# First mixer pass on unnormalized operands, with its outputs scaled, the weight folds inside the pass, and two reorderings

## The chip, the cores and the metric

One core of a Trainium2 chip runs the whole kernel. The metric is the device time of one execution in microseconds (us); smaller is better. The engines are TensorE (PE, with its weight load PEld), VectorE (DVE), ScalarE (ACT), GpSimd (POOL) and SyncE (SP, which here issues the DMA transfers).

## The reference

The kernel computes two layers over a sequence of 2048 rows of 1024 channels, in float32. Layer 0 mixes with a gated short convolution, layer 1 with causal window means in four groups; after each mixer comes a gated embedding of `p`, and one norm ends it.

```
def rmsnorm(x, g):
    r = lax.rsqrt(jnp.mean(xf * xf, axis=-1, keepdims=True) + EPS)
    return (xf * r) * g
def short_conv_mixer(h, w_in, w_conv, w_out):
    b_g, c_g, v, z = jnp.split(h @ w_in, 4, axis=-1)
    y = b_g * causal_conv3(c_g * v, w_conv)
    return (jax.nn.silu(z) * y) @ w_out
def pool_mixer(h, w_in, w_grp, scale, w_out):
    u, z = jnp.split(h @ w_in, 2, axis=-1)
    d = pooled - u4                      # causal means over 2, 4, 8, 16 rows, by group
    mixed = einsum('bsgc,gcd->bsgd', d, w_grp) * scale
    return (jax.nn.silu(z) * mixed) @ w_out
def reference(...):
    for i in range(DEPTH):               # DEPTH = 2
        hn = rmsnorm(h, norm_mix[i])
        h = h + mixer(hn, ...)           # i = 0: short_conv_mixer, i = 1: pool_mixer
        gate = sigmoid(rmsnorm(h, ple_norm[i]) @ ple_w_gate[i])
        h = h + gate * (p[i] @ ple_w_proj[i])
    return rmsnorm(h, final_norm)
```

## The kernel before

**Tiles.** Channels lie on the 128 partitions (8 tiles, `KT`), the sequence along the free dimension in four chunks of `T` = 512 rows. A pass (`sc`) takes two chunks through all stages, so there are two passes. `x` arrives twice in memory: `xT` with channels on partitions, `xN` with rows on partitions.

**Products.** A float32 product is made of three in a shorter form: weights and operands are each split into a high part (a cast on ACT: L116 for weights, L301 for operands) and the rest (a subtraction on DVE: L117, L302). The three matmuls are L273, L274 and L275, of 512 columns each. Operands that need only a channel gain are split by L307 (ACT) and L308 (DVE).

**The pair scheme.** In the mixers two chunks and two weight blocks are multiplied by seven products in place of eight. `Operands` holds the seven operand combinations (x11, x21, t2, t1, t3, x22, t4; four tiles each, 28 splits of 128x512); `pair_steps` is a generator of four steps (parts 0 to 3), whose PSUM results are copied by ACT (L428) and added by DVE (L433). `mixer_a` runs 8 output blocks `j`, each with a `cv` pair (the c and v projections) and a `zb` pair (z and b): 2 x 7 products of 12 matmuls, 168 matmuls per `j`. From c and v comes `u` (L484, DVE), then the convolution (one scale on ACT, L491, two DVE steps, L493, for each chunk), then sigmoid (L511), L512, L513 and `y` (L516).

**Weights.** They come in granules of 128x1024 (512 KB): `order` is the list of them as they will be asked for, `load_granule` issues the DMA on SP (L110) into `raw` (4 buffers), ACT and DVE split it into a weight ring (4 buffers), and `prefetch` keeps up to `LOOK` = 3 ahead (1 in the start). In the first pass the scheme's weight sums (L134 to L140 on DVE) are also written to memory, and `prepare_sums` makes those of the output weights (L548 on `n` tiles); the second pass loads them. Other pools: `wk` 10 tiles of 128x512 for elementwise work, `pm` 7 PSUM tiles, `acts` 31.

**The start.** The order in the program is: load chunk 0 of `xT`; sums of squares of chunk 0 (`square_sums`: ACT L328, DVE L331); the embedding products of chunks 0 and 1 (`ple_half`, 96 matmuls; each result is copied by ACT at L735 and stored by L736 to `pdr`); load chunk 1; `roots`; `fold` for groups 0 and 1 (a product of `w_grp` with the output weights, 48 matmuls of 256 columns for a group, 192 in all); squares of chunk 1 on PE with a matrix of ones (L879); the operands x11, x21 with their norm (`normed`, L545: gain and row factor `rb` in one DVE instruction); `fold` for groups 2 and 3; t2. Then `mixer_a` begins.

**The turn.** Between the passes, at the gates of layer 1, `X.ahead(1 + t)` splits operands of the second pass (their tiles `n` come back from memory, `ndr`), once after each gate block; `finals` writes outputs, and `filler` makes the embedding products of chunk 2 (eight L735 copies).

**What sets the order.** A scheduler fixes each engine's order when the program is built, by priority in program order; every engine then runs its list in order, and an instruction that waits holds up all behind it on its engine. The lines of `mixer_a` that the change touches:

```
cs1, cs2, v1, v2 = pair_of(cv_steps)
...                                    # u = c * v, then cv = conv(u)
z1, z2, b1, b2 = pair_of(zb_steps)     # takes the steps that are left
if j + 1 < KT:
    cv_steps = steps(j + 1, 0)
    next(cv_steps)
```

## Time and profile before

| what | value |
|---|---|
| median of 3 runs | 1846.69 us (1844.87 to 1856.14) |
| the profiled execution | 1848.54 us, its span 1846.8 us |
| mean granted TensorE clock | 0.991 of full speed |
| PE busy | 1776.5 us (96%), 8014 instructions |
| DVE busy | 1350.7 us (73%), 1878 instructions |
| ACT busy | 754.6 us (41%), 1141 instructions |
| POOL busy | 233.3 us (13%), 218 instructions |
| from memory, to memory | 225.49 MB, 97.52 MB |

The span counts from the first to the last instruction; 1.7 us of the profiled execution lie around it. The profiled execution is 1.9 us above the median. Busy matmuls overlap in the records, so a PE that is shown busy need not be at its full pace; the count of matmuls in a stretch says what it did.

### The profile page before, as it was taken

The page shows a single profiled execution, that of the slowest core. Times are in us where ns is not written, and L with a number is a line of the kernel's source. Part 1 is how long each engine was busy: PE and PEld are TensorE (multiplying, and loading weights), DVE is VectorE, ACT ScalarE, POOL GpSimd, SP SyncE. Part 2 cuts the span into 40 slices and gives each one's busy share as a digit, 9 for nine tenths or more (in the row PEclk, how much of TensorE's full clock was granted, in tenths as well). Part 3 has the DMA queues.
Part 4 walks back from the last instruction along what each step waited for, and adds up shares of the span by engine and source line. Part 5 has one row for each costly group of instructions (what it writes and reads, how often), then busy time and mean ns, then how long its engine had stood idle before and what let it go on. Part 6 is the DMA issues. An engine that isn't in the chain of part 4 may idle for free.

```text
span 1846.8 us, 22147 instructions
## 1 busy us (share of the span) xinstructions
PE 1776.5 (96%) x8014; PEld 1459.0 (79%) x8014; DVE 1350.7 (73%) x1878; ACT 754.6 (41%) x1141; POOL 233.3 (13%) x218
## 2 busy tenths in 40 slices
PE   8799999989999999999979999999999999999996
PEld 6587777878788888887868877877878888888796
DVE  4886776776988778879786555466698876578975
ACT  6642333344656221345553233234465511135542
POOL 1000000000322010013210000000032300001320
PEclk9999999999999999999999999999999999999998
DMA  9545455667355456853674434246635522265431
GB/s 322 191 146 195 168 205 186 243 232 272 114 194 187 146 198 221 281 198 127 209 239 155 137 103 137 94 146 221 246 126 194 192 109 99 97 224 170 142 114 47
DMA packets 122495, 324.49 MB, mean 176 GB/s; under 512 B 13584, under 2 KB 15632, under 8 KB 122384
## 3 DMA queue, kind: packets, MB, share of 16 engines
q1 hardware_dynamic: 122384, 323.06, 50.8%
q8 instruction: 63, 1.03, 0.2%
q14 instruction: 48, 0.39, 0.1%
HBM read 225.49 MB, written 97.52 MB: 175 GB/s over the span
## 4 chain that ended last, share of the span: by engine, by line
PE 65%; DVE 17%; issue 5%; DMA 5%; ACT 3%; POOL 1%; SPq 1%; DVEq 0%; ACTq 0%; POOLq 0%
PE mm L275 22%; PE mm L273 21%; PE mm L274 21%; DVE w L117 5%; DVE act L302 2%; DMA n<-ndr 2%; DMA n<-in_wts_dram 2%; DVE act L308 2%; ACT w L116 1%; DVE h L699 1%; DMA raw<-in_wts_dram 1%; DVE wk L754 1%; DVE n L548 1%; SPq L601 1%; ACT wk L428 1%
## 5 line engine op out<-in xcount | busy, mean ns | idle before, releaser
L273 PE MATMUL mm<-act,w 128*128 128x512 f32 (+1 forms) x2464 | 942.2, 385 | 19.5 <-ACT wk L428 10.8
L275 PE MATMUL mm<-act,w 128*128 128x512 f32 (+1 forms) x2464 | 935.0, 384 | 12.2 <-DVE w L117 12.0
L274 PE MATMUL mm<-act,w 128*128 128x512 f32 (+1 forms) x2464 | 943.7, 383 | 0.0
L273 PEld LDWEIGHTS mm<-act,w 128*128 128x128 f32 x2464 | 464.2, 188 | 121.3 <-ACT wk L428 16.6
L275 PEld LDWEIGHTS mm<-act,w 128*128 128x128 f32 x2464 | 463.2, 188 | 108.4 <-DVE w L117 17.7
L274 PEld LDWEIGHTS mm<-act,w 128*128 128x128 f32 x2464 | 464.4, 188 | 90.5 <-issue 0.5
L116 ACT CAST w<-raw 128x1024 fp32r<-128x1024 f32 (+1 forms) x283 | 281.6, 1002 | 563.2 <-PE mm L275 474.7
L117 DVE TENSOR_TENSOR w<-raw,w 128x1024 fp32r<-128x1024 f32 (+1 forms) x283 | 336.6, 1194 | 130.8 <-ACT w L116 127.2
L331 POOL TENSOR_TENSOR acc<-acc,wk 128x512 f32<-128x512 f32 x97 | 142.9, 1474 | 490.4 <-ACT wk L328 490.4
L433 DVE TENSOR_TENSOR wk<-mm,wk 128x512 f32<-128x512 f32 x96 | 65.8, 686 | 100.5 <-PE mm L275 100.5
L308 DVE SCALAR_TENSOR_TENSOR act<-h,par_sb,act 128x512 fp32r<-128x512 f32 x96 | 103.8, 1084 | 19.9 <-ACT act L307 17.9
L328 ACT ACTIVATE wk<-h 128x512 f32<-128x512 f32 (+1 forms) x126 | 75.3, 600 | 93.6 <-DVE h L755 93.2
L307 ACT ACTIVATE act<-h,par_sb 128x512 fp32r<-128x512 f32 x96 | 68.9, 718 | 72.7 <-DVE h L699 72.7
L699 DVE TENSOR_TENSOR h<-mm,h 128x512 f32<-128x512 f32 x112 | 75.9, 682 | 26.7 <-PE mm L275 20.7
L302 DVE TENSOR_TENSOR act<-n,act 128x512 fp32r<-128x512 f32 x112 | 76.3, 710 | 22.8 <-ACT act L301 22.7
L428 ACT COPY wk<-mm 128x512 f32<-128x512 f32 x96 | 53.0, 585 | 94.9 <-PE mm L275 94.9
L301 ACT CAST act<-n 128x512 fp32r<-128x512 f32 x112 | 65.7, 619 | 57.3 <-DMA n<-ydr 27.6
L669 DVE TENSOR_TENSOR wk<-wk 128x526 f32<-128x526 f32 (+5 forms) x80 | 55.5, 693 | 2.4
L352 POOL TENSOR_TENSOR r<-ms,nhalf 128x8 f32<-128x8 f32 x18 | 33.1, 1837 | 186.5 <-DVE ms L350 186.5
L684 ACT ACTIVATE wk<-wk 128x512 f32<-128x512 f32 x32 | 20.2, 630 | 78.0 <-DVE wk L682 77.9
L753 ACT ACTIVATE wk<-wk 128x512 f32<-128x512 f32 (+1 forms) x72 | 41.3, 579 | 21.6 <-DVE wk L752 21.4
L682 DVE TENSOR_TENSOR wk<-mm,rb 128x512 f32<-128x512 f32 x32 | 22.0, 688 | 37.6 <-PE mm L275 37.6
(124 smaller groups left out, 1296.1 us busy)
## 6 DMA issues: line engine op xcount, KB each, us to landing
raw<-in_wts_dram SPq DMA_DIRECT2D x154, 512.0 KB, 3.4
n<-ydr SPq DMA_DIRECT2D x84, 256.0 KB, 4.5
ydr<-y SPq DMA_DIRECT2D x32, 512.0 KB, 3.3
raw<-in_wts_dram SPq DMA_DIRECT2D x64, 256.0 KB, 3.3
raw<-sdo SPq DMA_DIRECT2D x32, 512.0 KB, 6.3
raw<-sda SPq DMA_DIRECT2D x32, 512.0 KB, 3.7
pdr<-wk SPq DMA_DIRECT2D x56, 256.0 KB, 4.0
n<-pdr SPq DMA_DIRECT2D x56, 256.0 KB, 3.5
```

Source lines behind the costliest of these rows:

```text
L116: nc.scalar.copy(out=hi[:, c], in_=raw[:, c])
L117: eng.tensor_tensor(out=lo[:, c], in0=raw[:, c], in1=hi[:, c].bitcast(F32), op=ALU.subtract)
L273: nc.tensor.matmul(out=ps, lhsT=wh, rhs=ah, start=first, stop=False, skip_group_check=skip)
L274: nc.tensor.matmul(out=ps, lhsT=wh, rhs=al, start=False, stop=False, skip_group_check=skip)
L275: nc.tensor.matmul(out=ps, lhsT=wl, rhs=ah, start=False, stop=last, skip_group_check=skip)
L302: nc.vector.tensor_tensor(out=a[:, 1, :], in0=y, in1=a[:, 0, :].bitcast(F32), op=ALU.subtract)
L307: nc.scalar.activation(out=a[:, 0, :], in_=h, func=AF.Copy, scale=pcol(gcol))
L308: nc.vector.scalar_tensor_tensor(out=a[:, 1, :], in0=h, scalar=pcol(gcol), in1=a[:, 0, :].bitcast(F32), op0=ALU.mult, op1=ALU.subtract)
L328: nc.scalar.activation(out=sq, in_=h, func=AF.Square)
L331: (eng or nc.gpsimd).tensor_tensor(out=acc, in0=acc, in1=sq, op=ALU.add)
L428: nc.scalar.copy(out=c, in_=ps)
L699: nc.vector.tensor_tensor(out=hs[t][k], in0=ps, in1=hs[t][k], op=ALU.add)
```

## The change

1. **The first pass runs on unnormalized operands.** They carry only the channel gains (`split_scaled`, and `gained`, which takes the place of a `normed` with a `vec`). The row factor is found by `row_stats(0)`: eight `xN` tiles of 512 KB are loaded, squared with an accumulating ACT instruction, and the factors are spread over the partitions by two matmuls. `rb` multiplies z and the convolution's result, and its square `rb2` multiplies c: six more DVE multiplications per `j`. The sums of squares, the roots and the products with ones at the start go.
2. **The folds** leave the start; `fold(g)` stands after the zb pair of `j` = 2, 3, 4, 5, and each loads three granules of its own.
3. **The z, b steps** (parts 0 and 1 of the zb pair) are asked for ahead of the convolution, in both passes.
4. **At the turn** `X.ahead(1)` stands in place of `X.ahead(1 + t)`: 16 of the 28 operands are split there, not 24.

The diff, cut:

```
--- before.py
+++ after.py
...
 HK = D // 2
+FOLDS = 3
 LAG = 3
...
+    def fold_order(g):
+        return [("w", W_GRP + g // 2), ("w", W_UT + 2 * g), ("w", W_UT + 2 * g + 1)]
     def sum_order(sc, n):
...
     order += ple_order(0, 0, "p", "pt") + [("p", 1)]
-    for g in range(4):
-        kind = "pt" if g < 2 else "w"
-        order += [("pt", W_GRP + g // 2)] if g % 2 == 0 else []
-        order += [(kind, W_UT + 2 * g), (kind, W_UT + 2 * g + 1)]
     for sc in range(2):
         order += filler_order(0, 2) if sc else []
-        order += sum_order(sc, 2 * KT)
+        order += sum_order(sc, 4)
+        for i in range(4, 2 * KT, 2):
+            order += fold_order(i // 2 - FOLDS) if sc == 0 and FOLDS <= i // 2 < FOLDS + 4 else []
+            order += [("sum", (sc, i + r, part)) for r in range(2) for part in range(4)]
         order += filler_order(0, 3) if sc else filler_order(1, 0)
...
-    def fold(g, wg, u):
+    def fold(g):
+        wg, *u = [next_granule(key) for key in fold_order(g)]
         for half in range(2):
...
                 look[0] = LOOK
+                if sc == 0:
+                    rb = list(row_stats(0))[-1]
+                    rb2 = []
+                    for t in range(2):
+                        rb2.append(rbp.tile([P, T], F32, tag="rb", name="rb2"))
+                        nc.scalar.activation(out=rb2[t], in_=rb[t], func=AF.Square)
             cs1, cs2, v1, v2 = pair_of(cv_steps)
...
                 u = wtile()
+                if sc == 0:
+                    vec(c, c, rb2[t], ALU.mult)
                 nc.gpsimd.tensor_copy(out=u[:, 0:2], in_=uh[:, j, :] if t == 0 else us[0][:, T:T + 2])
...
                 nc.gpsimd.tensor_copy(out=uh[:, j, :], in_=us[1][:, T:T + 2])
+            if j:
+                next(zb_steps)
+            next(zb_steps)
             cvs = []
...
             z1, z2, b1, b2 = pair_of(zb_steps)
+            if sc == 0 and FOLDS <= j + 1 < FOLDS + 4:
+                fold(j + 1 - FOLDS)
             if j + 1 < KT:
...
                 cv = cvs[t][:, :T]
+                if sc == 0:
+                    vec(z, z, rb[t], ALU.mult)
+                    vec(cv, cv, rb[t], ALU.mult)
                 zs = wtile()[:, :T]
...
-    def first_operand(x, stats):
+    def first_operand(x):
+        def gained(out, x, k, y, op):
+            nc.vector.scalar_tensor_tensor(out=out, in0=x, scalar=pcol(G_MIX + k), in1=y, op0=ALU.mult, op1=op)
         def make(name, kk):
-            n11, n12, n21, n22 = (x[t][2 * kk + r] for r in range(2) for t in range(2))
+            k1, k2 = 2 * kk, 2 * kk + 1
+            n11, n21 = x[0][k1], x[0][k2]
             if name == "x11":
-                normed(n11, n11, 2 * kk, stats[0].rb)
-                return split_act(n11)
+                return split_scaled(n11, G_MIX + k1)
             if name == "x21":
-                normed(n21, n21, 2 * kk + 1, stats[0].rb)
-                return split_act(n21)
+                return split_scaled(n21, G_MIX + k2)
+            n12, n22 = x[1][k1], x[1][k2]
+            if name == "x22":
+                return split_scaled(n22, G_MIX + k2)
             if name == "t2":
-                normed(n12, n12, 2 * kk, stats[1].rb)
-                normed(n22, n22, 2 * kk + 1, stats[1].rb)
-                vec(n12, n22, n12, ALU.subtract)
-                vec(n11, n12, n11, ALU.add)
-                return split_act(n11)
+                nc.scalar.activation(out=n12, in_=n12, func=AF.Copy, scale=pcol(G_MIX + k1))
+                gained(n12, n22, k2, n12, ALU.subtract)
+                gained(n11, n11, k1, n12, ALU.add)
             if name == "t1":
-                vec(n21, n21, n11, ALU.subtract)
-                vec(n11, n22, n11, ALU.subtract)
-                return split_act(n11)
-            return split_act({"t3": n12, "x22": n22, "t4": n21}[name])
+                gained(n21, n21, k2, n11, ALU.subtract)
+                gained(n11, n22, k2, n11, ALU.subtract)
+            return split_act({"t2": n11, "t1": n11, "t3": n12, "t4": n21}[name])
         return make
...
-    def square_sums(t):
...
-    def square_sums_pe(t):
...
-                nc.scalar.activation(out=sq[:, k - i, :], in_=x[t][k], func=AF.Square)
-                nc.tensor.matmul(out=tot, lhsT=ones_s, rhs=sq[:, k - i, :], start=k == 0, stop=k == KT - 1)
...
-    def roots(t):
...
-    def fold_next(g):
...
-    prefetch(2)
+    prefetch(3)
     load_chunk(0)
-    prefetch(3)
-    square_sums(0)
     pt = next_granule(("p", 0))
...
             pt = next_granule(("p", 1))
-    prefetch(8)
+    X = Operands(first_operand(x))
+    X("x11")
     load_chunk(1)
-    roots(0)
-    fold_next(0)
-    fold_next(1)
-    square_sums_pe(1)
-    X = Operands(first_operand(x, stats))
-    X("x11")
     X("x21")
-    fold_next(2)
-    fold_next(3)
     X("t2")
...
+    def row_stats(sc):
+        ssum = st.tile([P, 8], F32, tag="ssum", name="ssum")
+        for j in range(KT):
+            t = acts.tile([P, D], F32, tag="act", name="xr")
+            nc.sync.dma_start(out=t, in_=xN[sc * KT + j])
+            nc.scalar.activation(out=t, in_=t, func=AF.Square, accum_out=ssum[:, j:j + 1])
+            if j == KT - 1:
+                ms = st.tile([P, 8], F32, tag="ms8", name="ms8")
+                nc.vector.tensor_scalar(out=ms, in0=ssum, scalar1=1.0 / D, scalar2=EPS, op0=ALU.mult, op1=ALU.add)
+                r = st.tile([P, 8], F32, tag="r8", name="r8")
+                nc.gpsimd.tensor_tensor(out=r, in0=ms, in1=nhalf, op=ALU.pow)
+                yield spread(r, 0), spread(r, 4)
+            else:
+                yield
     rbs = []
+    row_steps = row_stats(1)
     def gather(j):
...
+        rbs.extend(next(row_steps) or ())
...
             if sc == 0:
-                X.ahead(1 + t)
+                X.ahead(1)
```

How this moves instructions, at three places. First SP's list in the start, in the embedding of chunk 1; `pdr_134` and `pdr_135` are stored embedding products, `h` is chunk 1 of `xT`, `s` and `sda` are weight sums and where they are stored, `xr` are the `xN` tiles. Before:

```order
L736 DMA pdr_134<-wk 128x512 x8
L736 DMA pdr_135<-wk 128x512 x3
L401 DMA h<-in_xT_dram 128x1024 x2
L736 DMA pdr_135<-wk 128x512 x3
L401 DMA h<-in_xT_dram 128x1024 x2
L736 DMA pdr_135<-wk 128x512 x2
L419 DMA wcomb_122<-wc 128x512
```

After:

```order
L759 DMA pdr_135<-wk 128x512
L404 DMA h<-in_xT_dram 128x1024 x2
L759 DMA pdr_135<-wk 128x512
L111 DMA raw<-in_wts_dram 128x1024
L183 DMA sda_145<-s_486 128x1024
L759 DMA pdr_135<-wk 128x512 x3
L187 DMA sda_145<-raw 128x1024
L759 DMA pdr_135<-wk 128x512 x3
L111 DMA raw<-in_wts_dram 128x1024
L909 DMA xr<-in_xN_dram 128x1024 x8
L111 DMA raw<-in_wts_dram 128x1024
```

The last two loads of chunk 1 stand behind nine stores (eight of `pdr_134` stand ahead of the rows shown) in place of fourteen, and the eight `xN` tiles behind all of these, behind the first stored sums and behind two granules of weights.

Second, ACT's list at the last `j` of the second pass; the casts of `w` split weights, those of `n` are operands of a later stage. Before:

```order
L301 CAST act<-n 128x512 x5
L116 CAST w<-raw 128x1024
L116 CAST w<-raw 128x512
L116 CAST w<-raw 128x1024
L491 ACTIVATE wk<-wk,par_sb 128x512 x2
L428 COPY wk<-mm 128x512 x3
L116 CAST w<-raw 128x1024 x2
L511 ACTIVATE wk<-wk 128x512 x2
L735 COPY wk<-mm 128x512
```

After:

```order
L304 CAST act<-n 128x512 x5
L117 CAST w<-raw 128x1024
L117 CAST w<-raw 128x512
L117 CAST w<-raw 128x1024
L432 COPY wk<-mm 128x512 x3
L506 ACTIVATE wk<-wk,par_sb 128x512 x2
L117 CAST w<-raw 128x1024 x2
L531 ACTIVATE wk<-wk 128x512 x2
```

The three PSUM copies (L428, now L432) now stand ahead of the two convolution scales (L491, now L506).

Third, ACT's list at the turn, at the first copies of the filler (L735, now L758); the casts of `n` are the splits of the second pass's operands, and L753 (L776) belongs to the gate. Before:

```order
L301 CAST act<-n 128x512
L328 ACTIVATE wk<-h 128x512
L301 CAST act<-n 128x512
L753 ACTIVATE wk<-wk 128x512
L301 CAST act<-n 128x512
L328 ACTIVATE wk<-h 128x512
L735 COPY wk<-mm 128x512 x4
L301 CAST act<-n 128x512 x2
```

After:

```order
L304 CAST act<-n 128x512 x2
L331 ACTIVATE wk<-h 128x512
L304 CAST act<-n 128x512
L776 ACTIVATE wk<-wk 128x512
L117 CAST w<-raw 128x1024
L304 CAST act<-n 128x512 x3
L331 ACTIVATE wk<-h 128x512
L758 COPY wk<-mm 128x512 x4
L304 CAST act<-n 128x512
L339 CAST acc_hi<-acc 128x512
L304 CAST act<-n 128x512
```

In the whole list 25 such casts stand ahead of the filler's first copy before, and 21 now; the others follow it.

## Rows read from the trace of the kernel before

**Rows 1.** Busy time of each engine, from the page.

```profile
PE 1776.5 (96%) x8014; PEld 1459.0 (79%) x8014; DVE 1350.7 (73%) x1878; ACT 754.6 (41%) x1141; POOL 233.3 (13%) x218
```

**Rows 2.** Windows by stage: length, busy (instructions) by engine, granted clock, DMA share, GB/s.

```profile
125.00:376.00 251.00, 242.00 (x1047) 194.84 (x1045) 179.62 (x258) 83.83 (x118) 17.39 (x19) 1.00 0.57 198
376.00:460.00 84.00, 80.15 (x351) 65.66 (x352) 59.08 (x78) 37.37 (x56) 2.81 (x3) 1.00 0.71 252
460.00:860.00 400.00, 397.73 (x1747) 327.17 (x1746) 331.31 (x456) 169.67 (x255) 78.59 (x68) 1.00 0.54 186
905.00:1000.00 95.00, 85.22 (x364) 68.75 (x363) 71.95 (x99) 46.23 (x73) 15.38 (x12) 0.98 0.67 220
1000.00:1237.00 237.00, 233.09 (x1017) 189.66 (x1016) 128.43 (x169) 76.69 (x109) 5.62 (x12) 1.00 0.37 121
1237.00:1276.00 39.00, 35.43 (x149) 28.60 (x148) 22.96 (x32) 14.80 (x23) 0.70 (x2) 0.96 0.53 182
...
700.00:800.00 100.00, 100.00 (x442) 82.63 (x441) 84.53 (x131) 27.04 (x39) 7.19 (x11) 1.00 0.74 263
```

**Rows 3.** Windows in the start, same columns.

```profile
0.00:25.00 25.00, 17.43 (x62) 12.16 (x63) 13.21 (x21) 16.62 (x24) 3.65 (x16) 0.93 0.88 321
...
0.00:125.00 125.00, 104.81 (x501) 82.95 (x502) 92.56 (x137) 74.92 (x129) 8.72 (x21) 0.95 0.64 228
...
37.00:47.00 10.00, 10.00 (x85) 9.96 (x84) 4.27 (x10) 5.59 (x15) 1.65 (x1) 1.00 0.96 355
86.00:93.00 7.00, 2.54 (x5) 1.59 (x6) 7.00 (x12) 5.52 (x9) 0.00 (x0) 0.53 0.37 150
```

**Rows 4.** Waits of PE, 0 to 125: total us, times, longest.

```profile
PE mm L275 <- DVE w L117: 6.3, 2, 3.2
PE mm L273 <- ACT wk L735: 4.0, 1, 4.0
```

**Rows 5.** Timeline of the start: when, how long, what, count [idle before].

```profile
7.20 0.50 PE L273 MATMUL mm<-act 128*128 128x512 f32 x1 [1.73 <-ACT act L116]
...
16.13 4.43 ACT L328 ACTIVATE wk<-h 128x512 f32<-128x512 f32 x7
...
53.33 1.88 PE L879 MATMUL mm<-sq,ones_s 128*128 128x512 f32 x4
...
63.27 1.64 POOL L352 TENSOR_TENSOR r<-ms,nhalf 128x8 f32<-128x8 f32 x1 [24.14 <-DVE ms L350]
...
74.06 2.49 DVE L548 TENSOR_TENSOR h<-h 128x512 f32<-128x512 f32 x4
...
112.94 0.69 DVE L484 TENSOR_TENSOR wk<-mm,wk 128x512 f32<-128x512 f32 x1 [1.12 <-PE mm L275]
```

**Rows 6.** DVE by line and form, 0 to 120: count, busy, mean ns, idle before.

```profile
L302 DVE TENSOR_TENSOR act<-h,act 128x512 fp32r<-128x512 f32 x28 | 17.8, 677 | 2.8 <-ACT act L301 2.8
...
L117 DVE TENSOR_TENSOR w<-raw,w 128x1024 fp32r<-128x1024 f32 x9 | 10.8, 1214 | 0.0
L545 DVE SCALAR_TENSOR_TENSOR h<-h,par_sb,rb 128x512 f32<-128x512 f32 x16 | 10.8, 747 | 4.2 <-ACT rb L364 4.2
```

**Rows 7.** The same: the costliest groups (page), then 120 to 380.

```profile
L308 DVE SCALAR_TENSOR_TENSOR act<-h,par_sb,act 128x512 fp32r<-128x512 f32 x96 | 103.8, 1084 | 19.9 <-ACT act L307 17.9
...
L548 DVE TENSOR_TENSOR n<-n 128x512 f32<-128x512 f32 x32 | 21.9, 686 | 10.8 <-DMA n<-in_wts_dram 10.5
```

**Rows 8.** Timeline at the last `j` of each pass.

```profile
393.02 1.33 ACT L491 ACTIVATE wk<-wk,par_sb 128x512 f32<-128x512 f32 x2
...
394.87 0.50 PE L273 MATMUL mm<-act,w 128*128 128x512 f32 x1 [2.16 <-ACT wk L428]
...
1267.87 0.79 PE L273 MATMUL mm<-act,w 128*128 128x512 f32 x1 [2.84 <-ACT wk L428]
...
1273.00 0.50 PE L273 MATMUL mm<-act,w 128*128 128x512 f32 x1 [0.73 <-ACT wk L428]
```

**Rows 9.** Timeline at the turn.

```profile
960.32 0.80 PE L273 MATMUL mm<-w 128*128 128x512 f32 x1 [5.08 <-ACT wk L735]
```

More of the change, by code (lines that the diff above doesn't have):

```diff
@@ L858, in trunk_kernel @@
     look[0] = 1
-    x, stats = [], []
+    x = []
     def load_chunk(t):
@@ L864, in load_chunk @@
             x[t].extend(both[:, i, :] for i in range(2))
-    def square_sums(t):
-        s = Stat()
-        for k in range(KT):
-            s.add(x[t][k], nc.vector)
-        stats.append(s)
-    def square_sums_pe(t):
-        s = Stat()
-        tot = psum()
-        for i in range(0, KT, 2):
-            sq = acts.tile([P, 2, T], F32, tag="act", name="sq")
-            for k in (i, i + 1):
-                nc.scalar.activation(out=sq[:, k - i, :], in_=x[t][k], func=AF.Square)
-                nc.tensor.matmul(out=tot, lhsT=ones_s, rhs=sq[:, k - i, :], start=k == 0, stop=k == KT - 1)
-        s.root(tot.rearrange("p (a b) -> p a b", b=64))
-        s.fin2()
-        stats.append(s)
-    def roots(t):
-        stats[t].fin1()
-        stats[t].fin2()
-    wg = []
-    def fold_next(g):
-        if g % 2 == 0:
-            wg.append(next_granule(("pt", W_GRP + g // 2)))
-        kind = "pt" if g < 2 else "w"
-        fold(g, wg[-1], [next_granule((kind, W_UT + 2 * g + c)) for c in range(2)])
-    prefetch(2)
+    prefetch(3)
     load_chunk(0)
-    prefetch(3)
-    square_sums(0)
     pt = next_granule(("p", 0))
@@ L906, in trunk_kernel @@
             pt = next_granule(("p", 1))
-    prefetch(8)
+    X = Operands(first_operand(x))
+    X("x11")
     load_chunk(1)
-    roots(0)
-    fold_next(0)
-    fold_next(1)
-    square_sums_pe(1)
-    X = Operands(first_operand(x, stats))
-    X("x11")
     X("x21")
-    fold_next(2)
-    fold_next(3)
     X("t2")
-    sums_n = const.tile([P, 8], F32, name="sums_n")
+    def row_stats(sc):
[12 more added lines that the diff above has]
+                yield
     rbs = []
+    row_steps = row_stats(1)
     def gather(j):
-        t = acts.tile([P, D], F32, tag="act", name="xr")
-        nc.sync.dma_start(out=t, in_=xN[j])
-        nc.scalar.activation(out=t, in_=t, func=AF.Square, accum_out=sums_n[:, j:j + 1])
-        if j == KT - 1:
-            ms = st.tile([P, 8], F32, tag="ms8", name="ms8")
-            nc.vector.tensor_scalar(out=ms, in0=sums_n, scalar1=1.0 / D, scalar2=EPS, op0=ALU.mult, op1=ALU.add)
-            r = st.tile([P, 8], F32, tag="r8", name="r8")
-            nc.gpsimd.tensor_tensor(out=r, in0=ms, in1=nhalf, op=ALU.pow)
-            rbs.extend([spread(r, 0), spread(r, 4)])
+        rbs.extend(next(row_steps) or ())
     def between_b(j):
@@ L1004 @@
     xT = chunks(x[0], KT)
-    xN = x[0, 2 * T:].reshape(KT, P, D)
+    xN = x[0].reshape(2 * KT, P, D)
     pT = np.stack([chunks(p[i, 0], 2) for i in range(2)]).reshape(2 * NCH, P, 2 * T)
```

## The prediction

> **What bounds the kernel now.** I read the totals first, then windows cut at the stages, then PE's waits and the timeline around the places that the change touches. PE is busy 96% of the span, DVE 73%, ACT 41% [rows 1]. Overlapping matmuls hide idle time, so I judge PE by counting. The densest 100 us hold 442 matmuls of 512 columns [rows 2], 0.2263 us each, and a stretch loses its length less its count times that pace: 14.1 us in 125 to 376 (1047 matmuls), 4.6 in 376 to 460, 4.8 in 460 to 860, 12.6 in 905 to 1000, 6.9 in 1000 to 1237 and 5.3 in 1237 to 1276 [rows 2]. Where PE runs at pace, only removed PE work shortens the kernel, and the change removes almost none: twelve statistic products out, two in. What there is to win is lost time, and the start has most of it. The folds alone run at 85 products of 256 columns in 10 us, 0.12 each [rows 3]. Up to 125.0 PE has 501 records [rows 3]: 10 for warming, 96 embedding products, 192 fold products, 20 records of the twelve statistic products, and therefore 183 products of the mixer. The first of them runs at 7.20 [rows 5]; at pace the rest are worth 21.7 + 23.0 + 8.6 (0.43 a record, four in 1.88 with an end of 0.6 [rows 5]) + 41.4, so they would end at 102, and 23 of the 125 us are lost, 6.3 of them in two waits for a weight split and 4.0 in one for an embedding copy [rows 4].
>
> **The start.** My landmark is the end of the 183rd mixer product, 125.0 before; the 23.0 us of folds in it come back later and are added at the end.
> - The first embedding product runs at 7.20 [rows 5]. The wait for the copies goes: seven squares on ACT, 4.43 us [rows 5], stood ahead of them and are removed. So 96 products end at 7.2 + 21.7 = 28.9.
> - The next 48 products (x11 and x21 with two weight blocks) need chunk 0 alone and only their splits: 39.8.
> - What follows needs chunk 1. By SP's order 10.75 MB stand up to its last tile; at the 321 to 355 GB/s of the stretches with full queues [rows 3] it lands at 30 to 33.5, and I take 31.7.
> - From there DVE sets the end. In its order, between the first `gained` and the second `u` product, stand 16 `gained` instructions, 16 operand splits, 4 gain splits, 19 other multiplications and sums of 128x512, 3 weight splits and 4 short pieces of the statistics. Back to back an instruction of 128x512 starts 0.60 after the one before (four in 2.49 us [rows 5], where one lasts 0.68), and I take the same 0.075 off the mean times of the others: 0.67 for L545's kind, 0.605 for L302, 1.14 for L117 [rows 6], 1.0 for L308 [rows 7]. That makes 10.7 + 9.7 + 4.0 + 11.5 + 3.4 + 1.4, about 41 us, so 72.7.
> - Into this the statistics come. 18.9 MB stand up to the last `xN` tile, so it lands at 53 to 59 by the same rates; then come its square (about 1 us, an estimate from ACT's casts of that size), a POOL power of 1.64 [rows 5], and spreading and squaring on PE and ACT. DVE meets the first of this at about 58 and the first multiplication by `rb2` some 6 us later. I allow 5 us of waiting: 78, where the second `u` stood at 112.9 [rows 5].
> - PE by then has run 156 mixer products and is out of PSUM tiles and `wk` tiles until `u` is made. 1.6 us later it goes on, and 27 more end at 85.7. With the folds' 23.0: 108.7. **The term is -16.3.**
> - Bounds. If DVE is never late, 28.9 + 183 x 0.2263 + 23.0 = 93.3, -31.7. If transfers run at the 228 GB/s of the whole start [rows 3], the last `xN` tile lands at 83, the second `u` comes at 91 and the landmark at 122, -3. I stand nearer to the fast rates, since these loads stand in an unbroken row of SP's list.
>
> **The rest of the first pass.** The folds run at the pace already charged, between zb pairs of `j` = 2 to 5. DVE gets six multiplications for each `j`, 42 after the landmark, 42 x 0.605 = 25.4 us, and 12 weight splits of the folds, 12 x 1.14 = 13.7: together 39.1. In 125 to 376 it was busy 179.6 of 251 us; with the new work and 23 us of folds it is (179.6 + 39.1) / 274 = 80%. The nearest stretch is 460 to 860, where DVE is busy 83% and PE loses 1.2% [rows 2]. So most of the new work fits beside PE: I charge 1.2% of 251, 3.0, and as much again for the two `j` that carry no fold but prepare output sums, where by count DVE has 37.7 us of work in 38 of PE. The `n` loads for which DVE waits 10.5 us [rows 7] remain. The wait of 2.16 behind two L491 scales (1.33 us) [rows 8] goes, because the copies now stand ahead of them. **The term is +4** (3.0 + 3.0 - 2.2). Bounds: at best the 14.1 lost now and the 2.2 are all regained, -16; at worst nothing of the 39.1 is hidden, +39.
>
> **The turn.** Four fewer splits, on ACT and DVE, stand ahead of the filler's copies, for which PE waits 5.08 us and then runs at half clock [rows 9]. The gate's own waits stay. Each split costs ACT about 0.6 us: 4 x 0.6 = 2.4, plus part of the slow stretch. **-3**, between 0 (the copy is late for its own input) and -12.6 (all that is lost there [rows 2]).
>
> **The second pass** has the same order with the z, b steps ahead, and no new work. At its last `j` the wait of 2.84 behind the two scales at 1267.87 falls away, with the slow clock behind it (0.79 us for a matmul of 0.50 [rows 8]; about 1.7 by count), the 0.73 at 1273.00 [rows 8], and shorter waits of the same kind in 1000 to 1237. **-6**, between 0 and -12.2 (6.9 + 5.3, all that is lost there).
>
> **Sum:** -16.3 + 4 - 3 - 6 = -21.3. The profiled execution took 1848.5, so 1827.2 on its basis, and 1825.3 on that of the median, which lies 1.9 lower.
>
> **The rivals.**
> - *DVE gives the gain back.* Half of the 39.1 us comes onto the path, because a DVE that is late frees PSUM tiles late, and then PE waits at each `j`: +19.6 in place of +4, 1841. For it: DVE already has 37.7 of 38 us in some blocks, and weights wait in the same list. Against: PE loses 1.2% beside a DVE at 83% [rows 2]. Chance 0.22.
> - *The clock falls in the start.* Before, the clock stood at about half in 86 to 93 (0.53, and 5 matmuls in 7 us [rows 3]), where PE met waits of up to 3.2 us [rows 4]. In the new start PE meets several short idle times between 40 and 78, waiting for DVE. Two half-clock stretches of 10 us run 22 products each less than at pace, 5 us each, and the sum becomes -11: 1835. Chance 0.13. The Trainium skill, "TensorE: Matmul & The Clock Gate", section "A second HAM failure mode: psum-queue depth-cycling", says that frequent short idle times between matmul groups make the clock swing between its levels and cost throughput; by that rule the new start would read like the 0.53 row, and the time would be this rival's; the mean clock of the old start, 0.95 over 125 us with several such idle times in it [rows 3], bears it out in part only.
> - *Slower: the folds stop DVE's cover.* A fold holds three of the four weight buffers, and its results pass through `raw` tiles. If the splits that follow can't run under it, the new 39.1 us stands wholly on the path: -16.3 + 39.1 - 9 = +13.8, 1860.5. It decides once more than 16.3 + 9 = 25.3 of the 39.1 reach the path. Against: a granule in the one free buffer feeds twelve products, 2.7 us, and DVE splits the next in 1.21 [rows 6] once ACT has cast it. With the start at its slow bound (-3) as well it ends at 1874. Chance 0.08.
> - *The start does better:* statistics and chunk 1 are early and DVE is never late, about -32 for the first term: 1810. Chance 0.07.
> - That the order doesn't change as written is excluded: the order of the changed kernel shows the copies ahead of the scales.
>
> **How the numbers follow.** The forecast has 0.50. Its own range is 1815 to 1836, from half of each term's reach. One per cent, 18.5 us, is about what a measurement of this kernel can tell: faster means under 1828.2, slower over 1865.2. Of the forecast's 0.50 some 0.36 lies under 1828.2, of the better start all 0.07, and of the first two rivals 0.12 (their other terms may come out better): 0.55. Slower is the last third of the third rival and some of the first: 0.06. The range, 1806 to 1845, leaves out 0.2: the slow rival, the upper part of the first, and the better start's own best.
>
> **What would show it.** Right: the second `u` product at 75 to 80; the mixer's 183 products done by 90 with no fold among them; no seven squares ahead of the first embedding copies; PE's waits of the first pass no longer than before; no wait for the copy at the last `j` of either pass; the filler's wait shorter by 2 to 3. Wrong: PE waiting for DVE at many `j` of the first pass; clock rows of 0.5 between 40 and 80; the spread products waited for past 80; the 5 us before the filler unchanged. The largest risk is the start, where one late transfer moves everything behind it.

## The result and the profile after

The changed kernel takes 1821.86 us, the median of 4 runs (1818.12 to 1824.92); the kernel before took 1847.76 in the same comparison. The ratio is 0.9844, with an interval of 0.9821 to 0.9867: 1.6% faster. The profiled execution took 1822.86 us, its span 1820.9, 25.9 us less than before. The page shows PE with almost the same work, and DVE with slightly more:

```profile
PE 1766.7 (97%) x7998; PEld 1457.0 (80%) x7998; DVE 1368.1 (75%) x1897; ACT 758.0 (42%) x1148; POOL 226.9 (12%) x217
```

Since all kernels here run the same 7248 products of 512 columns in nearly the same order, the traces can be laid side by side by product: when is the n-th one over? Numbers count from the first product of the mixer, behind the 96 embedding products; a numbered row gives the start of the product that follows the n-th, the first row and the last the start of the one that they name. The first column of numbers is read from the timeline of PE before, the second from that of the changed kernel.

| product | before | after | difference | the stage's own share |
|---|---|---|---|---|
| last of the 96 embedding products | 34.84 | 28.86 | -6.0 | |
| 183rd of the mixer | 125.14 | 86.70 | -38.4 | start, -38.4 + 23.0 of folds = **-15.4** |
| 1344th (first mixer pass over) | 406.94 | 385.72 | -21.2 | +17.2 - 23.0 of folds = **-5.8** |
| 3504th (ahead of the turn) | 906.33 | 885.01 | -21.3 | -0.1 |
| 3704th (behind the turn) | 965.20 | 940.60 | -24.6 | **-3.3** |
| 5104th (second mixer pass over) | 1295.82 | 1266.26 | -29.6 | **-5.0** |
| 7104th | 1757.20 | 1727.58 | -29.6 | 0.0 |
| the program's last but one matmul | 1838.14 | 1812.14 | -26.0 | **+3.6** |

The windows of the changed kernel (columns as in [rows 2]): the mixer's first pass from its 183rd product to its end; the middle, the turn and the two pieces of the second pass, cut at about the same products as those of before; and three of the start:

```profile
86.70:385.70 299.00, 290.01 (x1354) 240.15 (x1353) 239.35 (x339) 115.83 (x178) 13.51 (x21) 1.00 0.64 224
439.00:838.70 399.70, 397.43 (x1746) 327.09 (x1745) 331.64 (x456) 169.54 (x255) 78.19 (x68) 1.00 0.54 186
883.70:975.40 91.70, 84.40 (x364) 68.72 (x363) 74.75 (x100) 47.24 (x74) 15.74 (x12) 0.98 0.69 230
975.40:1210.00 234.60, 231.85 (x1016) 189.98 (x1015) 129.46 (x169) 76.64 (x109) 4.20 (x12) 1.00 0.36 120
1210.00:1247.00 37.00, 34.71 (x153) 28.09 (x152) 21.67 (x31) 14.90 (x23) 0.70 (x2) 1.00 0.59 206
50.00:60.00 10.00, 10.00 (x42) 8.14 (x41) 5.99 (x9) 10.00 (x20) 0.00 (x0) 0.93 0.85 323
43.00:50.00 7.00, 4.34 (x9) 2.53 (x10) 6.96 (x12) 4.34 (x8) 0.00 (x0) 0.61 1.03 413
60.00:70.00 10.00, 7.28 (x20) 4.28 (x19) 9.05 (x17) 6.86 (x12) 3.83 (x2) 0.83 0.23 83
```

The middle window takes as long as before to 0.3 us, 399.70 for 1746 matmuls in place of 400.00 for 1747: nothing moves where nothing was changed. In the start there are three things that a window of the whole would hide: from 43 to 50 DVE is full (6.96 of 7), PE runs 9 products and the clock is at 0.61; from 50 to 60 ACT is full (10.00 of 10) and DVE has only 5.99 us of work; and from 60 to 70 the clock falls again, to 0.83.

PE's waits up to 125, then from 86 to 390 with those of the kernel before from 125 to 410 under them, and then at the end, from 1670 on:

```profile
PE mm L277 <- DVE act L305: 3.9, 3, 2.4
PE mm L277 <- DVE act L311: 1.9, 2, 1.5
```

```profile
PE mm L276 <- ACT wk L432: 9.0, 10, 1.8
...
PE mm L273 <- ACT wk L428: 5.8, 8, 2.2
PE mm L275 <- DVE w L117: 5.7, 7, 2.1
```

```profile
PE tot L373 <- DVE acc L334: 5.0, 1, 5.0
PE tot L344 <- ACT acc_hi L339: 2.4, 1, 2.4
```

Of the two kinds of wait of [rows 4] the one for embedding copies is gone and 0.5 us is left of the one for weight splits; PE now waits for operand splits. In the first pass the waits for weight splits (5.7 us before) are gone as well, and copies alone are waited for, 9.0 us in place of 5.8. The timeline of the changed kernel at four places, the second `u` product, the last `j` of the first pass, the filler, and the last `j` of the second pass:

```profile
78.95 0.69 DVE L496 TENSOR_TENSOR wk<-mm,wk 128x512 f32<-128x512 f32 x1 [2.50 <-PE mm L278]
...
373.73 0.50 PE L276 MATMUL mm<-act,w 128*128 128x512 f32 x1 [1.85 <-ACT wk L432]
...
935.94 0.80 PE L276 MATMUL mm<-w 128*128 128x512 f32 x1 [4.52 <-ACT wk L758]
...
1239.78 0.50 PE L276 MATMUL mm<-act,w 128*128 128x512 f32 x1 [1.62 <-ACT wk L432]
...
1243.46 0.50 PE L276 MATMUL mm<-act,w 128*128 128x512 f32 x1 [0.67 <-ACT wk L432]
```

The second `u` comes at 78.95 in place of 112.94 [rows 5]. At the last `j` of the second pass the wait shrinks from 2.84 to 1.62 and, with that, the clock stays up (a matmul of 0.50 in place of 0.79 [rows 8]). The filler still waits, 4.52 in place of 5.08, and still runs its first products at half clock [rows 9].

### The profile page after: what moved, and what is told of

Its sections match the earlier page's. It is cut to its first block, busy times and chain, and to the rows that moved or that the text cites. A ratio compares the mean times of both kernels' runs of the same rounds, so it can differ in the third digit from the quotient of the medians.

```text
span 1820.9 us, 22137 instructions
## 1 busy us (share of the span) xinstructions
PE 1766.7 (97%) x7998; PEld 1457.0 (80%) x7998; DVE 1368.1 (75%) x1897; ACT 758.0 (42%) x1148; POOL 226.9 (12%) x217
## 4 chain that ended last, share of the span: by engine, by line
PE 72%; DVE 14%; DMA 5%; issue 5%; ACT 3%; POOL 1%; SPq 0%; DVEq 0%; ACTq 0%; POOLq 0%
PE mm L276 24%; PE mm L277 24%; PE mm L278 24%; DVE w L118 3%; DVE act L305 2%; DVE act L311 2%; DMA raw<-in_wts_dram 2%; ACT w L117 2%; DMA n<-ndr 2%; DVE h L722 1%; POOL r L355 1%; DVE wk L777 1%; DVE h L808 1%; DVE dg L360 0%; DVE h L574 0%
## 5 line engine op out<-in xcount | busy, mean ns | idle before, releaser
L276 PEld LDWEIGHTS mm<-act,w 128*128 128x128 f32 x2432 | 458.6, 189 | 115.8 <-ACT wk L432 16.9
L277 PEld LDWEIGHTS mm<-act,w 128*128 128x128 f32 x2432 | 458.2, 188 | 98.5 <-DVE act L305 5.8
L278 PEld LDWEIGHTS mm<-act,w 128*128 128x128 f32 x2432 | 458.1, 188 | 91.7 <-DVE w L118 1.0
L117 ACT CAST w<-raw 128x1024 fp32r<-128x1024 f32 (+1 forms) x291 | 289.2, 1002 | 525.4 <-PE mm L278 427.1
L118 DVE TENSOR_TENSOR w<-raw,w 128x1024 fp32r<-128x1024 f32 (+1 forms) x291 | 346.7, 1197 | 101.4 <-ACT w L117 98.5
L311 DVE SCALAR_TENSOR_TENSOR act<-h,par_sb,act 128x512 fp32r<-128x512 f32 x108 | 112.8, 1048 | 25.5 <-ACT act L310 24.8
L331 ACT ACTIVATE wk<-h 128x512 f32<-128x512 f32 (+1 forms) x119 | 71.2, 599 | 92.5 <-DVE h L778 92.5
L310 ACT ACTIVATE act<-h,par_sb 128x512 fp32r<-128x512 f32 x108 | 77.1, 719 | 75.9 <-DVE h L722 72.8
L432 ACT COPY wk<-mm 128x512 f32<-128x512 f32 x96 | 53.1, 589 | 84.2 <-PE mm L278 83.6
L508 DVE SCALAR_TENSOR_TENSOR wk<-wk,par_sb 128x512 f32<-128x512 f32 x64 | 44.1, 748 | 39.5 <-ACT wk L506 39.5
L276 PE MATMUL mm<-w 128*128 128x512 f32 (+1 forms) x144 | 48.8, 350 | 7.0 <-ACT wk L758 4.5
L776 ACT ACTIVATE wk<-wk 128x512 f32<-128x512 f32 (+1 forms) x72 | 41.3, 579 | 26.3 <-DVE wk L775 26.0
```

Of the source, the lines that this page charges most:

```text
L117: nc.scalar.copy(out=hi[:, c], in_=raw[:, c])
L118: eng.tensor_tensor(out=lo[:, c], in0=raw[:, c], in1=hi[:, c].bitcast(F32), op=ALU.subtract)
L276: nc.tensor.matmul(out=ps, lhsT=wh, rhs=ah, start=first, stop=False, skip_group_check=skip)
L277: nc.tensor.matmul(out=ps, lhsT=wh, rhs=al, start=False, stop=False, skip_group_check=skip)
L278: nc.tensor.matmul(out=ps, lhsT=wl, rhs=ah, start=False, stop=last, skip_group_check=skip)
L310: nc.scalar.activation(out=a[:, 0, :], in_=h, func=AF.Copy, scale=pcol(gcol))
```

## The experiments

My theory after the result: the start won by what was forecast; in the rest of the first pass, where I had forecast a loss, the z, b steps ahead of the convolution won. The rival: the folds between the pairs give weight splits time. All differences below are of the same product, against the changed kernel, from one profiled execution each; "timed" are the medians of four runs with their ratio to the kernel before and its 95% interval. Experiments 3, 8 and 11, which change nothing up to the 183rd product, have it from 1.0 earlier to 0.3 later than the changed kernel, so a difference of less than 1 us there says nothing.

**1. The z, b steps not ahead** (changed kernel), and **2. the z, b steps ahead alone** (kernel before).

```
-            if j:
-                next(zb_steps)
-            next(zb_steps)
             cvs = []
```

Experiment 2 adds the same three lines at the same place.

> The changed kernel without the z, b steps ahead of the convolution, in both passes. Stages are compared by when the same matmul runs. My theory (the steps ahead take the convolution scales out of the copies' way, and that is most of what the first pass after the start won): the second pass takes 5.0 us more than in the changed kernel, with waits of about 2.8 and 0.7 at its last j back; the first pass after its 183rd product takes 5 to 10 us more, so about 1832 to 1837. Rival (the folds between the pairs give weight splits time, and that won the 5.8 us there): the first pass is within 2 us of the changed kernel, only the second gives back 5, so about 1827.

> The kernel before with the z, b steps ahead alone. My theory: the second pass wins 5.0 us and the first pass after its 183rd product 5 to 10 us, start and turn unchanged: 1832 to 1838. Rival (folds): the second pass alone wins, 1842.

Measured: experiment 1 is timed 1839.22 (0.9932, 0.9912 to 0.9953). Its 183rd product is 1.2 late, its 1344th 12.3, its 5104th 18.3: the first pass gives back 11.2 and the second, with 0.7 at the turn, 6.0. Experiment 2 is timed 1834.74 (0.9906, 0.9883 to 0.9928); against the kernel before its first pass wins 7.8 and its second 5.0. Its turn is 0.6 longer than before's. The theory holds on both kernels, and in the first the price was above its range. ACT's timeline shows the mechanism; first the changed kernel, then experiment 1, at the same `j`:

```profile
148.16 1.05 ACT L117 CAST w<-raw 128x1024 fp32r<-128x1024 f32 x1 [3.64 <-PE mm L278]
149.12 0.58 ACT L432 COPY wk<-mm 128x512 f32<-128x512 f32 x1
152.79 1.07 ACT L432 COPY wk<-mm 128x512 f32<-128x512 f32 x2 [3.10 <-PE mm L278]
153.75 1.35 ACT L506 ACTIVATE wk<-wk,par_sb 128x512 f32<-128x512 f32 x2
```

```profile
149.34 1.05 ACT L117 CAST w<-raw 128x1024 fp32r<-128x1024 f32 x1 [3.64 <-PE mm L278]
150.29 1.33 ACT L503 ACTIVATE wk<-wk,par_sb 128x512 f32<-128x512 f32 x2
151.53 0.56 ACT L432 COPY wk<-mm 128x512 f32<-128x512 f32 x1
```

In experiment 1 the copy that frees a PSUM tile stands behind the weight cast and two scales, in the changed kernel behind the cast alone. So each `j` with a fold takes 1.2 us longer. That makes 4.8 of the 11.2. Most of the rest, 7.3, falls on one `j`, the seventh (products 1008 to 1176), where output sums stand in DVE's list and PE waits 3.7 us for weight splits; the eighth is 1.0 shorter. Experiment 1's waits of PE from 88 to 398:

```profile
PE mm L276 <- ACT wk L432: 13.1, 11, 2.2
PE mm L278 <- DVE w L118: 3.7, 2, 2.3
```

On the kernel before the places are others: the second to the sixth `j` win 0.7 to 2.8 us each and the last 2.0, and the seventh loses 2.5. The edit moves the whole convolution, two scales on ACT and four steps on DVE, and asks for two granules earlier; that the copies come earlier is seen, which of these makes the seventh `j` long was not tried.

**3. X.ahead as before** (changed kernel).

```
-                X.ahead(1)
+                X.ahead(1 + t)
```

> The changed kernel with X.ahead(1 + t) at the turn as before. My theory: the turn gives back its 3.3 us and nothing else moves, about 1825. Rival (the turn's gain comes from the earlier stages having another phase there, not from the four splits): the turn stays within 0.5 us of the changed kernel.

Measured: a single run, 1825.96. Against the changed kernel it is 0.5 late at product 2504 and 5.6 at 3704, so the gates and the turn take 5.1 more, where the kernel before took 3.3 more; nothing behind it moves up to the 7104th product. Behind that it takes 2.4 less than the changed kernel (see the end, below), so its profiled time is 3.1 longer. PE's waits around the turn, of the kernel before (905 to 1000), then of the changed kernel (883 to 976):

```profile
PE mm L273 <- ACT wk L735: 5.1, 1, 5.1
PE mm L273 <- DVE wk L752: 3.8, 2, 2.0
...
PE mm L276 <- ACT wk L758: 4.5, 1, 4.5
PE mm L276 <- DVE wk L775: 2.4, 1, 2.4
```

The wait for the gate's step on DVE (L752, now L775), which the changed kernel has once, comes twice in experiment 3 (3.5), as before, and the filler's wait is 4.8 in place of 4.5. The splits are the cause: from the 3504th product to the 3704th the four kernels with 24 splits at the turn (the one before and experiments 2, 3 and 5) take 58.9 to 60.3, and the ten with 16 take 54.2 to 56.1. The rival, another phase of the earlier stages, is out: experiment 3 has those of the changed kernel.

**4. The folds in the start** (changed kernel), and **5. the folds in the mixer** (kernel before).

```
     load_chunk(1)
+    fold(0)
+    fold(1)
     X("x21")
+    fold(2)
+    fold(3)
     X("t2")
...
             z1, z2, b1, b2 = pair_of(zb_steps)
-            if sc == 0 and FOLDS <= j + 1 < FOLDS + 4:
-                fold(j + 1 - FOLDS)
```

In experiment 5 the calls of `fold_next` at the start of the kernel before go, and the two lines that are taken out above are added. In both the list `order` follows.

> The changed kernel with its folds at the start, two after the load of chunk 1 and two after x21, each with three granules of its own; none in the mixer. My theory (DVE sets the start's end, and PE idles some 14 us of it): folds fill the idle time in part, but their 12 granules delay chunk 1 and add 14 us of weight splits to DVE, so the 183rd product comes at 110 to 118 and the mixer after it loses 23.9 us less: total 1820 to 1830, near the changed kernel. Rival (moving the folds is what won the start): the start ends near 125, as before, and the total is 1836 or more.

> The kernel before with its folds moved into the mixer's first pass at the same places as in the changed kernel; operands stay normalized and the rest is as before. My theory (moving the folds pays only together with unnormalized operands, since without folds PE has nothing to do while the norm of chunk 0 and 1 is made; the reverse was seen with unnormalized operands and the folds left in the start, where the 183rd mixer product came at 124.2, 0.9 earlier than before): the 183rd product comes at 105 to 112 without folds, so the start with its 23.0 us of folds later is 3 to 13 us worse or no better than 125.1, and the total is within 1842 to 1856. Rival (moving the folds alone wins the start): 183rd product at 90 or earlier, total about 1835.

Measured: experiment 4 is timed 1827.73 (0.9873, 0.9854 to 0.9892). Its 183rd product comes at 124.20, later than I expected and 0.9 before that of the kernel before; and the rest of its first pass is 29.3 shorter than the changed kernel's, 6.3 more than the folds' 23.0. So unnormalized operands with the folds left in the start won next to nothing there: PE waits for the folds' weights instead, which have to be loaded and cast (PE's waits, 28 to 125):

```profile
PE mm L277 <- ACT w L117: 22.5, 3, 11.2
PE mm L277 <- ACT wc L422: 1.1, 1, 1.1
```

This holds for folds that are loaded as in the changed kernel, twelve granules through the weight ring. The kernel before loads ten, keeps six of them in tiles of `acts` and asks for five ahead of chunk 1's load; its PE waits 1.6 us for a weight of a fold. What unnormalized operands would win with the folds loaded in that way was not tried.

Experiment 5 is timed 1867.39 (1.009, 1.0074 to 1.0107): moving the folds alone makes the kernel slower. Its 183rd product comes at 107.33, inside the expected range; with the folds' 23.0 that is 5.2 worse than before, since PE then waits for the normed operands (28 to 125):

```profile
PE mm L276 <- ACT act L304: 15.6, 3, 11.1
PE mm L277 <- DVE act L305: 2.1, 2, 1.7
```

The total is worse than expected, because its first pass also loses 21.0 against the changed kernel's, 11.2 of which experiment 1 explains by the steps that aren't ahead; the other 9.8 stay open. In these kernels the start's 15.4 comes with both edits only: one makes PE's work of the mixer ready early, the other takes away what stood in its place, and either alone leaves PE waiting.

**6. No statistics, 7. no multiplications, 10. statistics not multiplied in, 12. loads without squares** (changed kernel; the first pass isn't normalized in these).

In experiment 6 `rb` and `rb2` are tiles filled with ones and `row_stats(0)` isn't called; in 10 it is called and a tile of ones stands for both. Experiment 7 leaves out the multiplications:

```
-                    vec(c, c, rb2[t], ALU.mult)
...
-                    vec(z, z, rb[t], ALU.mult)
-                    vec(cv, cv, rb[t], ALU.mult)
```

Experiment 12 changes `row_stats`:

```
+            if sc:
                 nc.scalar.activation(out=t, in_=t, func=AF.Square, accum_out=ssum[:, j:j + 1])
+            else:
+                nc.gpsimd.tensor_scalar(out=ssum[:, j:j + 1], in0=t[:, 0:1], scalar1=0.0, scalar2=float(D), ...)
```

> The changed kernel without the row statistics of its first pass: no xN loads, squares, power or spreading, rb and rb2 are set to one by a fill (so the first pass isn't normalized). My theory (in the start ACT's eight squares, 1.06 us each, hold up the splits for which DVE waits, and the spreading holds up the first u, together the 5 us that I allowed): the 183rd product comes 3 to 8 us earlier than 86.7, the rest is unchanged, 1814 to 1819. Rival (DVE's own work sets the start, the statistics are hidden): less than 1 us.

> The changed kernel without the six DVE multiplications for each j of the first pass (its outputs stay unnormalized); the statistics are still made. My theory (beside a DVE that is 80% busy they are hidden, and what PE waits for there is copies on ACT): the first pass after the 183rd product takes 0 to 3 us less, the start 0 to 2. Rival (DVE is the bound of the first pass, and 25 us of work cost a good part of themselves): 8 us less or more.

> The changed kernel with its row statistics made as they are, but multiplied in nowhere: a tile of ones stands in for rb and rb2 (the first pass isn't normalized). It tells the two ways apart in which the statistics cost 8.2 us. Theory A (ACT's squares and the 4 MB of loads hold up the splits): the 183rd product comes within 2 us of 86.7. Theory B (the first u waits for the spread factors): it comes 6 us or more earlier, as without statistics (78.5). Between, both.

> The changed kernel with its eight xN tiles loaded as they are, but not squared by ACT: POOL reads one column of each tile and writes a constant for its sum, and the factors are made and multiplied in as before (so the first pass isn't normalized). It splits what the statistics cost in the start (8.2 us, of which 2.3 go when the factors aren't multiplied in). Theory A (ACT's squares, 8 x 1.06 us in front of the casts): the 183rd mixer product comes 3 us or more earlier than 86.7, at 78.5 to 83.5. Theory C (the 4 MB of loads, with the DMA queues full until 50, delay chunk 1 and the weights): it comes within 1.5 us of 86.7.

Measured, by the 183rd product: experiment 6 -8.2, experiment 10 -2.3, experiment 12 -7.3. (Single runs: 1809.23, 1822.98 and 1814.24, and 1820.16 for experiment 7. Of the 2.3 of experiment 10 only 0.8 is left at the 3704th product.) So what the statistics cost in the start is ACT's squares, by what they hold up: the factors, whose late arrival costs 2.3, and the casts. The 4 MB of loads and all the rest of the statistics cost about 0.9 (8.2 - 7.3), which is within the scatter at this place. The windows of 50 to 60 show it; the row of the changed kernel stands above (ACT 10.00, DVE 5.99), and this one is of experiment 12:

```profile
50.00:60.00 10.00, 9.99 (x43) 7.88 (x43) 9.87 (x16) 7.63 (x12) 3.19 (x6) 0.98 0.85 324
```

With the same DMA load, DVE goes from 5.99 to 9.87 of 10 us. In the changed kernel the squares stand between the casts on ACT whose results DVE waits for:

```profile
54.58 1.06 ACT L910 ACTIVATE xr<-xr 128x1024 f32<-128x1024 f32 x1
55.53 0.20 ACT L910 ACTIVATION_READ_ACCUMULATOR xr<-xr 128x1 f32 x1
55.62 1.14 ACT L304 CAST act<-h 128x512 fp32r<-128x512 f32 x2
56.65 1.07 ACT L910 ACTIVATE xr<-xr 128x1024 f32<-128x1024 f32 x1
```

```profile
56.27 1.30 DVE L305 TENSOR_TENSOR act<-h,act 128x512 fp32r<-128x512 f32 x2 [2.26 <-ACT act L304]
58.35 0.69 DVE L305 TENSOR_TENSOR act<-h,act 128x512 fp32r<-128x512 f32 x1 [0.78 <-ACT act L304]
```

Experiment 7 is -1.0 at the 183rd product and -0.9 at the 1344th: the 42 multiplications between them, 25 us of DVE work, cost the first pass nothing. DVE, busy 239 of 299 us there, had the room.

**8. Each fold one step later, 11. one step earlier** (changed kernel).

```
             z1, z2, b1, b2 = pair_of(zb_steps)
-            if sc == 0 and FOLDS <= j + 1 < FOLDS + 4:
-                fold(j + 1 - FOLDS)
             if j + 1 < KT:
                 cv_steps = steps(j + 1, 0)
                 next(cv_steps)
+            if sc == 0 and FOLDS <= j + 1 < FOLDS + 4:
+                fold(j + 1 - FOLDS)
```

```
+            if sc == 0 and FOLDS <= j + 1 < FOLDS + 4:
+                fold(j + 1 - FOLDS)
             z1, z2, b1, b2 = pair_of(zb_steps)
-            if sc == 0 and FOLDS <= j + 1 < FOLDS + 4:
-                fold(j + 1 - FOLDS)
```

> The changed kernel with each fold one step later: behind the first step of the next cv pair in place of ahead of it (its granules are asked for in that order). My theory (the four folds cost 6.3 us beside their products, seen as waits of 1.1 and 0.8 for copies at each j that has one, because a copy stands behind a weight cast that waits for a ring buffer the fold holds): with the step's copies made under the fold these waits shrink, 3 to 7 us less, 1815 to 1819. Rival (the ring is held wherever the fold stands, or the waits belong to the place): the waits move and the time is within 1.5 us of the changed kernel.

> The changed kernel with each fold one step earlier: ahead of the last step of the zb pair in place of behind the pair (its granules are asked for in that order). A fold later cost 13 us. My theory (behind the pair the fold delays the copies that the next pair's first products need, 2.4 us beyond its products at each fold, 9.7 in all; the earlier place has the pair's own results still in PSUM, three tiles more than at its end, so PE's tiles run short): 0 to 10 us slower than the changed kernel. Rival (the fold covers the convolution and the copies): the four folds cost 5 us less, 1817.

Measured: experiment 8 is timed 1834.38 (0.9917, 0.9902 to 0.9932), 12.7 late at the 1344th product: my theory of the waits was wrong, as was the rival that nothing would change. Experiment 11 is timed 1840.45 (0.9952, 0.9933 to 0.9971), 20.0 late there, twice the worst that I expected. The copies' waits shrank, as I had meant, from 9.0 to 5.1 in experiment 8 and to 0.7 in 11, and waits for weight splits took their place; first experiment 8, then 11 (from 86 to 400 and to 407):

```profile
PE mm L279 <- DVE w L118: 7.4, 3, 2.5
PE mm L277 <- ACT wk L433: 5.1, 2, 4.4
PE mm L277 <- ACT w L117: 2.0, 4, 0.5
```

```profile
PE mm L278 <- ACT w L117: 10.5, 7, 2.1
PE mm L280 <- DVE w L118: 9.9, 4, 3.1
PE mm L278 <- ACT wk L434: 0.7, 1, 0.7
```

Between the pairs a `j` with a fold takes 2.4 us beyond its products at pace (products 336 to 504 take 46.2; at pace 38.0 + 5.75), with the fold between steps of a pair 3 to 5 more. Not all of the 2.4 is the fold's: by experiment 4, which has none there, the four folds cost the first pass 6.3 beyond their products. Why weights come later there was not tried; that three of the ring's four buffers hold the fold's granules while a pair is open would fit.

**9. The casts of t3 and t4 on POOL** (changed kernel).

```
-        nc.scalar.copy(out=a[:, 0, :], in_=y)
+        (nc.gpsimd.tensor_copy if pool else nc.scalar.copy)(out=a[:, 0, :], in_=y)   # pool: t3, t4
```

> The changed kernel with the eight casts of t3 and t4 in the first pass made by POOL (nearly idle there) in place of ACT. My theory (leaving out the statistics won 8.2 us of the start because ACT, busy throughout 50 to 60 with the squares, makes DVE wait 5 us for its casts): 4.9 us of ACT work less, so the 183rd mixer product comes 2 to 5 us earlier than 86.7 and the total is 1817 to 1820. Rival (the wait for the spread factors holds the first u, whatever ACT does; and a cast on POOL takes twice as long): not earlier, or up to 3 us later.

Measured: 1820.75 (0.9844, 0.9820 to 0.9868), the ratio of the changed kernel; its 183rd product at 86.98. Neither better nor worse, against my theory. Four of the casts taken away did wait behind the squares (ACT makes five in 50 to 60 in the changed kernel and one here), and DVE's waits for casts fall from 3.0 to 0.5. But DVE then waits 2.4 for a weight's cast, which stands on ACT behind a copy that waits for PE, and PE runs 38 products in 50 to 60, at a granted clock of 0.82, in place of 42 at 0.93. POOL takes 5.87 for its four casts there where ACT takes 0.62 for each. So freeing these casts alone is not enough; in experiment 12, without the squares, DVE waits 0.6 in all up to 80.

## Why the prediction was right, and where not

The forecast was 1825.3 with -21.3 on the profiled time; measured were 1821.9 and -25.7.

- **The start, -16.3 forecast, -15.4 measured.** The steps came nearly as written: embedding products over at 28.9 (their last one starts at 28.86), 48 products at 39.8 (39.97), the second `u` at 78 (78.95), the 183rd product at 85.7 (86.70). DVE's list without waiting was forecast to end at 72.7, and without the squares the second `u` comes at 72.53 (experiment 12); that agrees although chunk 1 landed at 34.6 and not at 31.7. The 5 us for the statistics were 6.4 by the same two times, and not for the reason given. I charged them to the wait for the factors, which costs 2.3 (experiment 10); the larger part is what ACT's squares hold up, 7.3 at the 183rd product with the factors in it (experiment 12). I had counted DVE's list without looking at what ACT has between the casts that feed it.
- **The rest of the first pass, +4 forecast, -5.8 measured.** This is the term that was mis-sized, by the reordering. I credited it with 2.2, the one long wait at the last `j`; it is worth 11.2 in this pass (experiment 1; 7.8 on the kernel before). I priced the wait that was seen in the trace of before, and not the place of the convolution ahead of a copy at every `j`. The 6.0 charged for DVE's new work came out in size and not in kind: the multiplications, 25.4 of the 39.1 us, cost nothing (experiment 7), and the folds cost 6.3 beyond their products (experiment 4). 6.3 - 11.2 makes -4.9 of the -5.8. By pace the first pass still loses 13.3 of its 299.0 us (299.0 - 1161 x 0.2263 - 23.0): 9.7 at the four `j` with a fold, and about 3.3 at the last, whose wait of 1.85 (2.16 before) I had expected to go.
- **The turn, -3 forecast, -3.3 measured**, by the splits (experiment 3), but not where I had put it; that the size agrees is luck. I expected the filler's wait for its copies to shrink by 2 to 3 and the gate's own waits to stay. The filler's wait shrank by 0.6, and the ten products up to it take 0.1 less. Of the 3.3, 0.9 is won in the gate (products 3552 to 3576) and 2.1 at the filler's wait for the gate's step on DVE (3672 to 3680), which came twice before and comes once now.
- **The second pass, -6 forecast, -5.0 measured.** The long wait shrank from 2.84 to 1.62 and did not go; the slow clock behind it went, and the last `j` takes 2.7 less. The rest comes from shorter waits at the other `j`. Experiment 2 finds the same 5.0 on the other kernel.
- **The end, not forecast, +3.6.** PE's order there is the same in both kernels. One granule whose load SP issues at the same point (1758.04 before, 1728.52 after) lands 5.25 us after its issue in place of 3.17, the chain behind it is late, PE waits 2.4 us for a statistic (0.2 before) and then runs at a granted clock of 0.63 for 4 us (1.00 before). In all fourteen profiled executions this load takes 3.17 to 5.25, and the stretch from the 7104th product to the last but one matmul 80.9 to 84.6, in nearly the same order; the kernel before has the shortest of both and the changed kernel the longest. So the +3.6 belongs to these two executions and not to the change. Why the load's time scatters stays open.

Without the end's scatter the sum would have been -29.3, 8.0 from the forecast, by the rest of the first pass.

Of the rivals, DVE giving the gain back did not come true (experiment 7), nor did the folds stop DVE's cover as a whole. The clock did fall in the start, as its rival said and as my signs of being wrong name it: 0.61 in 43 to 50 and 0.83 in 60 to 70, with 0.50 in 46 to 50, each time behind waits of PE for operand splits (up to 2.4 us). The rule of the Trainium skill, "TensorE: Matmul & The Clock Gate", section "A second HAM failure mode: psum-queue depth-cycling", agrees with these rows as far as the clock goes down and up again. The first fall lies where DVE is full and PE waits for it, and the start's size came out without a charge for it; what the falls cost was not measured by itself. That the gain is tied to several edits at once I had not considered: the folds moved with normalized operands and without the z, b steps ahead made the kernel 0.9% slower (experiment 5).

## What to carry to other kernels

In a list that an engine runs in order, look for short work that nobody waits for ahead of work that frees a buffer, at every turn of the loop and not only where the trace shows a long wait: taking the convolution, with two scales of 0.66 us on ACT, from in front of the copies won 13 us alone (experiment 2, by product) and cost 17 when undone (experiment 1). When DVE is the bound of a stretch, read what stands between the instructions of the engine that feeds it. While DVE waits it shows as idle (5.99 busy of 10), and work sent to the feeder because it has room on average can be paid for nearly in full, as the eight squares of 1.06 us were with 7.3. Removing a cover (the folds) and removing what it covered (the norm) were one edit here: the first alone was a loss (experiment 5), and the second alone won 0.9 of the start's 15.4 (experiment 4). And where a forecast's size comes out, check that the wait it named is the one that shrank.

## What was not expected of the hardware

Casts of 128x512 from float32 took POOL 0.61 to 1.07 us each in experiment 9, and the first one 3.28, where ACT takes 0.62. A load of 512 KB issued at the same point of the program landed 3.17 to 5.25 us later, depending on the execution, and the latest landing went with 3.6 us at the end, for PE also ran at a granted clock of 0.63 for 4 us behind the wait.
